# Weight sums of feed-forward groups 2 and 3: from beside group 1 into the second branch's projection

## The chip, the cores and the metric

One core of a Trainium2 chip runs the whole program. The metric is the device time of one execution in microseconds (us). TensorE (PE) multiplies, VectorE (DVE) and ScalarE (ACT) work on rows in on-chip memory, GpSimd (POOL) and SyncE (SP) issue transfers (DMAs) from queues of their own. The engines run side by side and wait for each other through semaphores.

## The reference

The reference is one block of a network on 256 tokens of width 2048, in 32-bit floats. What matters here, cut down:

```python
proj = x @ w_in                       # projections of both branches and two gates
o_a = gated_delta_rule_chunked(...)   # first branch
o_b = dsa_sparse_attention(...)       # second branch
merged = sigmoid(gate_a) * (o_a @ w_branch_a) + sigmoid(gate_b) * (o_b @ w_branch_b)
x = layer_norm(ALPHA * x + merged @ w_out)
h_gate, h_up = split(x @ w_ffn_in)    # 2048 x 11264
x = layer_norm(ALPHA * x + (silu(h_gate) * h_up) @ w_ffn_out)
```

## The kernel before

Every matrix product is made of three products of shortened numbers: a weight chunk of 128 x 1024 (512 KB) is loaded (`raw`), ACT makes its rounded part `hi` (L91), DVE the rest `lo = raw - hi` (L93), and `mm3` (L217 to L219) issues hi, lo and hi against the two parts of the activations, 512 columns each. `chunk` keeps four buffers each of `raw`, `hi` and `lo`.

Two K-tiles (a pair `q`) of a 1024-wide group of output columns form a 2 x 2 block product. `plain_pair` issues its 8 products (24 matmuls). `seven_pair` issues 7 (21 matmuls) in the manner of Strassen and Winograd: it needs sums of the activations (`f_form[q]`, made by `x_form`) and four sums of the weight blocks t1 to t4. Without prepared sums DVE makes them on the spot (`sum13`, L246; `sum24`, L250 and L251) and ACT and DVE split them (`thi`, `tlo`, L241 and L242). Where sums were prepared (`ready`), only one and a half chunks of the pair are left to load and split. After the last seven pair of a group, `sums_chain` (L1065 to L1072) reads the four shared accumulator banks (`wbank`) out, and the banks pass to the next group as its own four.

The first layers run in this order: projections, branch chains, `z_group`, four gate groups. Between the second and the third gate group stands the second branch's projection: four blocks of four chunks of `wbb`, twelve matmuls for each chunk. The feed-forward input layer is a first group 0 in two blocks (`wfi`) and ten groups of eight pairs (`x_group` on `wfg[i - 1]`, i from 1 to 10). `FQ[i - 1]` names the seven pairs of group i.

PE and SP run in program order. ACT, DVE and POOL are ordered by a scheduler from priorities: `high_priority(offset=LEAD)` moves work ahead, `offset=-LEAD` behind. Side work is written as generators ("chains"). `tick()` stands after each chunk or half pair and takes each chain to its next `yield`; the number yielded is how many ticks it rests. So a chain's SP transfers lie between the chunk loads of the tick in which they are issued.

Two chains prepare weight sums of pair 0 for the feed-forward groups:

- `kept_chain` (L941) makes those of groups 4 to 7 early in the program, with work behind everything else, writes them to DRAM (`d_s`) by POOL, and `kept_load` (L1407) brings each group's sums back while the group before it runs.
- the last part of `f_forms_chain` (L1385 on, `near`) makes those of groups 2 and 3 while group 1 starts, loads the raw weights, sums and splits them with ordinary priority, and keeps them on chip.

Group 1 itself has two seven pairs, 4 and 6, in the order 0 to 7. Groups 2 to 7 have four each, in the order `FO`.

Of the kernel before, what the change touches and what calls it, by code (L numbers as in the profile page):

```python
# [43 lines left out]
ZO = (0, 1, 3, 2, 4, 5, 6, 7)  # L44
OQ = (0, 2, 4, 6)
WALL = sorted({*WQ[0], *WQ[1]})
KEPT = (4, 5, 6, 7)
NEAR = (2, 3)
FQ = ((4, 6), *[(0, 2, 4, 6) if i in KEPT + NEAR else (2, 4, 6) for i in range(2, 11)])
FO = (1, 3, 2, 0, 4, 5, 6, 7)  # L50
KEPT_FROM = 56
OUT_AT = (8, 9, 10)
# [11 lines left out]
def block_kernel(ctx: ExitStack, tc: tile.TileContext, xT, x, cpack, onehot, relb, convw, alog, dtb, gnw,  # L64
# [35 lines left out]
    def start(gen, at_once=False):  # L100
        chains.append([gen, clock[0] + (next(gen) if at_once else 0)])
# [17 lines left out]
    def event(name):  # L119
        done[name] = clock[0]  # L120
# [86 lines left out]
    def split(hi, lo, src):  # L207
        nc.scalar.copy(hi, src)
        nc.vector.tensor_sub(lo, src, hi.bitcast(F32))
# [131 lines left out]
    def T(name, shape, dtype=F32, tag=None):  # L341
        return p1.tile(shape, dtype, name=name, tag=tag or name)
# [62 lines left out]
    def need(*names):  # L405
        for n in names:
            assert n in done, n
# [522 lines left out]
    def four_sums(ra, rb, lead=0):  # L930

        r0, r1, s0, s1 = (t[:, n * 512:n * 512 + 512] for t in (ra, rb) for n in range(2))
        with tc.high_priority(offset=lead):
            nc.vector.tensor_add(r0, r0, s1)
            nc.vector.tensor_add(s1, r1, s1)
        yield 1
        with tc.high_priority(offset=lead):
            nc.vector.tensor_add(r1, r0, r1)
            nc.vector.tensor_add(s0, r1, s0)

    def kept_chain():  # L941
        yield KEPT_FROM
        raws = [T("k_raw", [P, 2, 1024], tag=t) for t in ("oh_", "s_x")]
        hi = T("k_hi", [P, 2, 1024], F32R, tag="ol_")
        for m, g in enumerate(KEPT):
            raw = raws[m % 2]
            for i in range(2):
                nc.sync.dma_start(raw[:, i], wfg[g - 1, i])
                yield 1
            yield 1  # L950
            for _ in four_sums(raw[:, 0], raw[:, 1], -LEAD):
                yield 1
            yield 1
            for i in range(2):
                with tc.high_priority(offset=-LEAD):
                    for n in range(2):
                        cs = slice(n * 512, n * 512 + 512)
                        nc.scalar.copy(hi[:, i, cs], raw[:, i, cs])
                        nc.vector.tensor_sub(raw[:, i, cs].bitcast(F32R), raw[:, i, cs], hi[:, i, cs].bitcast(F32))
                yield 1  # L960
                nc.gpsimd.dma_start(d_s[m, 0, :, i], hi[:, i].bitcast(F32))
                nc.gpsimd.dma_start(d_s[m, 1, :, i], raw[:, i])
        event("kept")

    start(kept_chain())
    conv_first(s_kT, pss)
    event("kc0")
    for dst, h0, c0, ev in ((s_kT, 4, 12, "kc1"), (s_qT, 0, 0, "qc0"), (s_qT, 4, 4, "qc1"),
# [24 lines left out]
    def z_chain():  # L993

        yield "v1"
        yield 1
        need("kept")
        t0 = [rp.tile([P, 2, 1024], F32R, name=f"z_t{i}", tag=f"x1_{i}") for i in range(2)]
        wt = two("z_wt", F32, "ol_")
        gates_home.update(wraw=halves(two("z_wraw", F32, "oh_")), wt=halves(wt), thi=halves(t0[0]), tlo=halves(t0[1]))  # L1000
        for q, old in ((4, "s_ak"), (6, "s_sq")):
            t = T(f"g_form{q}", [P, 2, 4, P], F32R, tag=old)
            gates_form[q] = t[:, 0], t[:, 1]
        gates_form[2] = [p1.tile([P, 4, P], F32R, name="g_form2", tag="rel", bufs=2) for _ in range(2)]
        yield from early_sums(wz, ZQ[0], home, z_ready)
        yield 1
        x_form(ZQ[0], gates_form[ZQ[0]], wt[:, 0, :512], wt[:, 0, 512:])
        yield "lg"
        t1 = two("z_t2", F32R, "s_vT"), two("z_t3", F32R, "s_t")
        for tag, *t in zip(("thi", "tlo"), t0, t1):  # L1010
            gates_home[tag] = halves(*t)
            gates_home[tag][0] = 2
        yield from early_sums(wz, ZQ[1], home, z_ready)
        for q in ZQ[1:]:
            yield 1
            x_form(q, gates_form[q], wt[:, 0, :512], wt[:, 0, 512:])
        event("zready")
# [25 lines left out]
    def early_chain(src, qs, ready, ev):  # L1043
        for q in qs:
            yield from early_sums(src, q, home, ready)
        event(ev)

    def next_sets(*olds):
        for tag, old in zip(("thi", "tlo"), olds):
            e = gates_home[tag]  # L1050
            gates_home[tag] = [0, e[1][:2] + halves(two("h_" + old, F32R, old))[1]]
# [88 lines left out]

    def ga_rows():
        if "a" not in g_rows:
            next_sets("s_x", "s_mn")
            g_rows["a"] = [rp.tile([P, D], F32, name=f"ga{tb}", tag=f"x1_{tb}") for tb in range(NTB)]
        return g_rows["a"]
# [14 lines left out]
    for tag in ("thi", "tlo"):  # L1160
        gates_home[tag][0] = 0
    start(early_chain(wgt[2], (2, 4), ga_ready, "gaready"))
    for j in range(4):
        js = slice(j * 512, (j + 1) * 512)
        for tb, ps in enumerate(block_xs([wbb[j, k] for k in range(4)], *out_hl, ps_acc if j == 2 else ps_aux)):
            nc.vector.tensor_mul(gb[tb][:, js], ps, gb[tb][:, js])
# [72 lines left out]
    def h_tile(pool, i):  # L1239
        hH[i], hL[i] = (pool.tile([P, 4, S], F32R, name=f"{hl}{i}", tag=f"{hl}{i}") for hl in ("hH", "hL"))  # L1240
# [11 lines left out]
    def fetch(i, j):  # L1252
# [1 line left out]
        nc.sync.dma_start(t.rearrange("p k t -> p (k t)").bitcast(F32), d_h[i, j])  # L1254

    h_first = passing()
    near = [[hp_.tile([P, 1024], F32R if i > 1 else F32, name="near", tag=f"{hl}{i}") for hl in ("hH", "hL")]
            for i in range(1, 5)]
    l1 = ExitStack()
    gp = l1.enter_context(tc.tile_pool(name="gp1", bufs=1, side="left", reuse_waits="tile"))  # L1260
    ex = l1.enter_context(tc.tile_pool(name="ex1", bufs=4, side="left", reuse_waits="tile"))
# [93 lines left out]
                  lambda tb, ps: start(h_chain(0, tb, gated(tb, ps), ps_aux)))  # L1355
    l1.close()
    hp2 = fh.enter_context(tc.tile_pool(name="hp2", bufs=1, side="left", reuse_waits="tile"))
    near.append([hp2.tile([P, 1024], F32R, name="near", tag=f"{hl}5") for hl in ("hH", "hL")])
    kept = [None, [hp2.tile([P, 1024], F32R, name="kept", tag=f"{hl}6") for hl in ("hH", "hL")]]


    f_home = {}
# [13 lines left out]
    def f_forms_chain():  # L1376
        yield "x1"
        for tb in range(NTB):
            yield 2
            nc.sync.dma_start(d_x1[tb], x1[tb])  # L1380
        t = [rp.tile([P, 2, 2, 4, P], F32R, name="f_form", tag=f"x1_{tb}") for tb in range(NTB)]
        for i, q in enumerate((4, 6, 2, 0)):
            yield 1
            f_form[q] = t[i // 2][:, i % 2, 0], t[i // 2][:, i % 2, 1]
            x_form(q, f_form[q], fv(), fv())  # L1385
        yield 1
        raw = near[0]
        for m, g in enumerate(NEAR):
            for i in range(2):
                nc.sync.dma_start(raw[i], wfg[g - 1, i])  # L1390
                yield 1
            yield 1
            yield from four_sums(*raw)
            for i in range(2):
                yield 1
                split(near[1 + 2 * m][i], near[2 + 2 * m][i], raw[i])
            k_ready[g][0] = sums_of(near[1 + 2 * m], near[2 + 2 * m])
            yield 4

    k_ready = {g: {} for g in KEPT + NEAR}  # L1400

    def sums_of(hi, lo):
        (t1, t2), (t4, t3) = ([(hi[i][:, n * 512:n * 512 + 512], lo[i][:, n * 512:n * 512 + 512]) for n in range(2)]
# [3 lines left out]
    def kept_load(m):  # L1407

        for i in range(2):
            if m or not i:  # L1410
                kept[i] = [hp2.tile([P, 1024], F32R, name="kept", tag=f"{hl}{5 + i}") for hl in ("hH", "hL")]
            for j in range(2):
                if i or j:
                    yield 3
                nc.sync.dma_start(kept[i][j].bitcast(F32), d_s[m, j, :, i])
        k_ready[KEPT[m]][0] = sums_of(*zip(*kept))

# [47 lines left out]
    for i in range(1, NG + 1):  # L1465
        std, shared = (ps_aux, ps_acc) if i % 2 else (ps_acc, ps_aux)
        sums = []

        def places():
            sums.extend(fv() for _ in range(4))  # L1470
            return sums

        at = {6: lambda: start(kept_load(KEPT.index(i + 1)))} if i + 1 in KEPT else {}
        ready = k_ready.get(i)
        if ready is not None:
            at[0] = lambda ready=ready: ready[0]
        bank = x_group(wfg[i - 1], FQ[i - 1], std, shared, f_form, fhome, lambda wbank: sums_chain(places(), wbank),
                       at, range(8) if ready is None else FO, {} if ready is None else ready)
        if i == NEAR[-1]:
            for k in range(1, 5):  # L1480
                h_tile(hp_, k)
        if i == KEPT[-1]:
            for k in (5, 6):
                h_tile(hp2, k)
        if i == NG:
            h_tile(hp2, 7)
        start(hidden_chain(i, bank, sums, std), at_once=True)
# [258 lines left out]
```

## Time and profile before

| what | value |
|---|---|
| median of three runs (lowest, highest) | 1455.73 us (1454.38, 1456.3) |
| the profiled execution: its own time, its span | 1454.49 us, 1452.7 us |
| granted TensorE clock | 0.999 |
| PE, DVE, ACT busy, share of the span | 99%, 88%, 56% |
| moved from and to HBM | 312.88 MB read, 22.22 MB written |

The span goes from the first to the last instruction. A row of grouped instructions names the line, the engine, what is written and read, the count, the busy time and the mean time of one. A row of a tile gives minimum, median and maximum, and the first and the last start. In the timeline each row begins with the start and the duration in us, and a bracket gives the engine's idle time ahead of the instruction and what ended it. A matmul of 512 columns is shown as 0.39 us long, but they overlap: what counts is the distance between their starts.

### The profile page before, as it was taken

The page shows a single profiled execution, that of the slowest core. Times are in us where ns is not written, and L with a number is a line of the kernel's source. Part 1 is how long each engine was busy: PE and PEld are TensorE (multiplying, and loading weights), DVE is VectorE, ACT ScalarE, POOL GpSimd, SP SyncE. Part 2 cuts the span into 40 slices and gives each one's busy share as a digit, 9 for nine tenths or more (in the row PEclk, how much of TensorE's full clock was granted, in tenths as well). Part 3 has the DMA queues.
Part 4 walks back from the last instruction along what each step waited for, and adds up shares of the span by engine and source line. Part 5 has one row for each costly group of instructions (what it writes and reads, how often), then busy time and mean ns, then how long its engine had stood idle before and what let it go on. Part 6 is the DMA issues. An engine that isn't in the chain of part 4 may idle for free.

```text
span 1452.7 us, 19640 instructions
## 1 busy us (share of the span) xinstructions
PE 1443.7 (99%) x7140; PEld 1213.8 (84%) x7140; DVE 1279.0 (88%) x1763; ACT 813.9 (56%) x1021; POOL 56.2 (4%) x75
## 2 busy tenths in 40 slices
PE   9999999999999999999999999999999999999998
PEld 8888888888888888888888878888888888888887
DVE  6798988789699959998886999989999998989987
ACT  5765454557456646655435665656566565554552
POOL 0002011121000000000000000000000000000000
PEclk9999999999999999999999999999999999999999
DMA  8646589854556755756856767777766666887863
GB/s 293 197 159 196 175 216 335 295 187 151 169 198 232 233 193 198 247 188 204 304 202 218 264 236 253 251 271 255 279 211 212 216 215 247 311 342 265 315 215 118
DMA packets 101969, 336.40 MB, mean 232 GB/s; under 512 B 17696, under 2 KB 18888, under 8 KB 101360
## 3 DMA queue, kind: packets, MB, share of 16 engines
q1 hardware_dynamic: 88512, 310.03, 62.0%
q0 software_dynamic: 6176, 22.75, 4.6%
q10 hardware_dynamic: 7184, 2.36, 0.7%
q8 instruction: 56, 0.92, 0.2%
q14 instruction: 41, 0.34, 0.1%
HBM read 312.88 MB, written 22.22 MB: 231 GB/s over the span
## 4 chain that ended last, share of the span: by engine, by line
PE 92%; DVE 3%; DMA 3%; issue 1%; ACT 1%; SPq 0%; POOLq 0%; DVEq 0%; ACTq 0%
PE acc L217 10%; PE acc L218 10%; PE acc L219 10%; PE acc L153 10%; PE aux L218 9%; PE aux L217 9%; PE aux L219 9%; PE acc L156 5%; PE acc L175 3%; PE acc L173 3%; PE acc L174 3%; PE aux L173 2%; PE aux L174 1%; PE aux L175 1%; DMA raw<-in_win_dram 1%; PE aux L737 1%
## 5 line engine op out<-in xcount | busy, mean ns | idle before, releaser
L91 ACT CAST hi<-raw 128x1024 fp32r<-128x1024 f32 (+1 forms) x388 | 396.9, 1032 | 345.3 <-PE acc L219 87.3
L93 DVE TENSOR_TENSOR lo<-raw,hi 128x1024 fp32r<-128x1024 f32 (+1 forms) x388 | 463.5, 1205 | 87.3 <-ACT hi L91 84.7
L153 PE MATMUL acc<-X,hi 128*128 128x512 f32 x640 | 203.7, 400 | 0.0
L217 PE MATMUL acc<-hi,X 128*128 128x512 f32 x369 | 145.0, 393 | 0.8 <-DVE v L1072 0.8
L156 PEld LDWEIGHTS acc<-X,lo 128*128 128x128 f32 x640 | 120.2, 188 | 28.3
L219 PE MATMUL acc<-hi,X 128*128 128x512 f32 x369 | 143.7, 389 | 0.0
L218 PE MATMUL acc<-lo,X 128*128 128x512 f32 x369 | 143.6, 389 | 0.0
L156 PE MATMUL acc<-X,lo 128*128 128x256 f32 x640 | 126.0, 278 | 0.0
L217 PE MATMUL aux<-hi,X 128*128 128x512 f32 x313 | 122.4, 391 | 0.0
L219 PE MATMUL aux<-hi,X 128*128 128x512 f32 x313 | 121.9, 389 | 0.0
L218 PE MATMUL aux<-lo,X 128*128 128x512 f32 x313 | 121.8, 389 | 0.0
L153 PEld LDWEIGHTS acc<-X,hi 128*128 128x128 f32 x640 | 97.5, 189 | 2.0 <-ACT hi L91 0.7
L241 ACT CAST f_thi<-f_wt 128x1024 fp32r<-128x1024 f32 x58 | 61.0, 1053 | 46.4 <-DVE f_wt L251 23.9
L217 PEld LDWEIGHTS acc<-hi,X 128*128 128x128 f32 x369 | 69.3, 188 | 15.9 <-DVE v L1072 1.2
L219 PEld LDWEIGHTS acc<-hi,X 128*128 128x128 f32 x369 | 69.3, 188 | 14.5
L218 PEld LDWEIGHTS acc<-lo,X 128*128 128x128 f32 x369 | 69.3, 188 | 13.9
L242 DVE TENSOR_TENSOR f_tlo<-f_wt,f_thi 128x1024 fp32r<-128x1024 f32 x58 | 70.6, 1220 | 6.2 <-ACT f_thi L241 6.1
L219 PEld LDWEIGHTS aux<-hi,X 128*128 128x128 f32 x313 | 58.8, 188 | 12.3
L218 PEld LDWEIGHTS aux<-lo,X 128*128 128x128 f32 x313 | 58.8, 188 | 12.1
L217 PEld LDWEIGHTS aux<-hi,X 128*128 128x128 f32 x313 | 58.8, 188 | 12.0
L241 ACT CAST thi<-wt 128x1024 fp32r<-128x1024 f32 x36 | 37.9, 1054 | 49.0 <-DVE wt L246 31.6
L173 PE MATMUL acc<-hi,X 128*128 128x512 f32 x160 | 64.3, 402 | 0.0
(681 smaller groups left out, 3123.6 us busy)
## 6 DMA issues: line engine op xcount, KB each, us to landing
raw<-in_wfg_dram SPq DMA_DIRECT2D x125, 512.0 KB, 4.8
raw<-in_wws_dram SPq DMA_DIRECT2D x80, 512.0 KB, 4.1
raw<-in_wfo_dram SPq DMA_DIRECT2D x70, 512.0 KB, 5.0
raw<-in_wgt_dram SPq DMA_DIRECT2D x49, 512.0 KB, 3.9
f_wraw<-in_wfg_dram SPq DMA_DIRECT2D x29, 512.0 KB, 6.2
raw<-in_win_dram SPq DMA_DIRECT2D x21, 512.0 KB, 4.1
wraw<-in_wfo_dram SPq DMA_DIRECT2D x18, 512.0 KB, 5.1
gt<-d_g SPq DMA_DIRECT2D x18, 512.0 KB, 6.8
```

The source lines that it names most:

```text
L91: nc.scalar.copy(hi, raw)
L93: nc.vector.tensor_sub(lo, raw, hi.bitcast(F32))
L153: nc.tensor.matmul(pss[c], hv[:, kk, cs[c]], X2[k // 4][:, k % 4], start=(k == 0), stop=False, skip_group_check=True)
L156: nc.tensor.matmul(pss[c][:, :S], lv[:, kk, cs[c]], xh[:, k, :], start=False, stop=(k == KT - 1), skip_group_check=True)
L173: nc.tensor.matmul(ps, xh, hv[:, kk], start=(k == 0), stop=False)
L174: nc.tensor.matmul(ps, xh, lv[:, kk], start=False, stop=False)
L175: nc.tensor.matmul(ps, xl, hv[:, kk], start=False, stop=(k == 2 * n - 1))
L217: nc.tensor.matmul(o, sh, hi, start=first, stop=False)
L218: nc.tensor.matmul(o, sh, lo, start=False, stop=False)
L219: nc.tensor.matmul(o, sl, hi, start=False, stop=last)
L241: nc.scalar.copy(hi, v)
L242: nc.vector.tensor_sub(lo, v, hi.bitcast(F32))
```

## The change

`NEAR` goes; groups 2 and 3 join `KEPT`. `kept_chain` is started twice: for groups 4 to 7 as now, except that the list has become `range(2, 8)` and so the first start makes groups 2 to 5 (`m` from 0 to 3), and a second start makes groups 6 and 7 (`m` 4 and 5) in the second branch's projection. So six groups' sums go through `d_s`. The second start has one raw buffer (`s_x`), puts the rounded part into `s_rv`, and rests 5 ticks between its two groups. `kept_load` now brings in groups 2 to 7, the first during group 1. The `near` part of `f_forms_chain` and its tiles go. Group 1 gets pair 2 as a third seven pair and the order `F1`.

```diff
-KEPT = (4, 5, 6, 7)
-NEAR = (2, 3)
-FQ = ((4, 6), *[(0, 2, 4, 6) if i in KEPT + NEAR else (2, 4, 6) for i in range(2, 11)])
+KEPT = range(2, 8)
+FQ = [(0, 2, 4, 6) if i in KEPT else (2, 4, 6) for i in range(1, 11)]
+F1 = (1, 3, 4, 5, 6, 0, 2, 7)
...
-    def kept_chain():
-        yield KEPT_FROM
-        raws = [T("k_raw", [P, 2, 1024], tag=t) for t in ("oh_", "s_x")]
-        hi = T("k_hi", [P, 2, 1024], F32R, tag="ol_")
-        for m, g in enumerate(KEPT):
-            raw = raws[m % 2]
+    def kept_chain(ms, wait, old, old_hi, gap, ev):
+        yield wait
+        raws = [T(f"k_raw{t}", [P, 2, 1024], tag=t) for t in old]
+        hi = T(f"k_hi{old_hi}", [P, 2, 1024], F32R, tag=old_hi)
+        for m in ms:
+            if gap and m > ms[0]:
+                yield gap
+            raw = raws[m % len(old)]
             for i in range(2):
-                nc.sync.dma_start(raw[:, i], wfg[g - 1, i])
+                nc.sync.dma_start(raw[:, i], wfg[KEPT[m] - 1, i])
...
-    start(kept_chain())
+    start(kept_chain(range(4), KEPT_FROM, ("oh_", "s_x"), "ol_", 0, "kept0"))
...
     start(early_chain(wgt[2], (2, 4), ga_ready, "gaready"))
+    start(kept_chain(range(4, 6), 1, ("s_x",), "s_rv", 5, "kept1"))
...
-    near = [[hp_.tile([P, 1024], F32R if i > 1 else F32, name="near", tag=f"{hl}{i}") for hl in ("hH", "hL")]
-            for i in range(1, 5)]
+    for i in range(1, 5):
+        h_tile(hp_, i)
...
-        raw = near[0]
-        for m, g in enumerate(NEAR):
-            for i in range(2):
-                nc.sync.dma_start(raw[i], wfg[g - 1, i])
-                yield 1
-            yield 1
-            yield from four_sums(*raw)
-            for i in range(2):
-                yield 1
-                split(near[1 + 2 * m][i], near[2 + 2 * m][i], raw[i])
-            k_ready[g][0] = sums_of(near[1 + 2 * m], near[2 + 2 * m])
-            yield 4
...
         bank = x_group(wfg[i - 1], FQ[i - 1], std, shared, f_form, fhome, lambda wbank: sums_chain(places(), wbank),
-                       at, range(8) if ready is None else FO, {} if ready is None else ready)
+                       at, F1 if i == 1 else range(8) if ready is None else FO, {} if ready is None else ready)
```

The check that the sums have been written moves too: what follows in the first branch needs `kept0`, the third gate group's rows need `kept1`.

More of the change, by code (lines that the diff above doesn't have):

```diff
@@ L962, in kept_chain @@
                 nc.gpsimd.dma_start(d_s[m, 1, :, i], raw[:, i])
-        event("kept")
-    start(kept_chain())
+        event(ev)
+    start(kept_chain(range(4), KEPT_FROM, ("oh_", "s_x"), "ol_", 0, "kept0"))
     conv_first(s_kT, pss)
@@ L996, in z_chain @@
         yield 1
-        need("kept")
+        need("kept0")
         t0 = [rp.tile([P, 2, 1024], F32R, name=f"z_t{i}", tag=f"x1_{i}") for i in range(2)]
@@ L1142, in ga_rows @@
         if "a" not in g_rows:
+            need("kept1")
             next_sets("s_x", "s_mn")
@@ L1357, in block_kernel @@
     hp2 = fh.enter_context(tc.tile_pool(name="hp2", bufs=1, side="left", reuse_waits="tile"))
-    near.append([hp2.tile([P, 1024], F32R, name="near", tag=f"{hl}5") for hl in ("hH", "hL")])
-    kept = [None, [hp2.tile([P, 1024], F32R, name="kept", tag=f"{hl}6") for hl in ("hH", "hL")]]
+    kept = [[hp2.tile([P, 1024], F32R, name="kept", tag=f"{hl}{5 + i}") for hl in ("hH", "hL")] for i in range(2)]
     f_home = {}
@@ L1385, in f_forms_chain @@
             x_form(q, f_form[q], fv(), fv())
-        yield 1
-        raw = near[0]
-        for m, g in enumerate(NEAR):
-            for i in range(2):
-                nc.sync.dma_start(raw[i], wfg[g - 1, i])
-                yield 1
-            yield 1
-            yield from four_sums(*raw)
-            for i in range(2):
-                yield 1
-                split(near[1 + 2 * m][i], near[2 + 2 * m][i], raw[i])
-            k_ready[g][0] = sums_of(near[1 + 2 * m], near[2 + 2 * m])
-            yield 4
-    k_ready = {g: {} for g in KEPT + NEAR}
+    k_ready = {g: {} for g in KEPT}
     def sums_of(hi, lo):
@@ L1409, in kept_load @@
         for i in range(2):
-            if m or not i:
+            if m:
                 kept[i] = [hp2.tile([P, 1024], F32R, name="kept", tag=f"{hl}{5 + i}") for hl in ("hH", "hL")]
@@ L1477, in block_kernel @@
         bank = x_group(wfg[i - 1], FQ[i - 1], std, shared, f_form, fhome, lambda wbank: sums_chain(places(), wbank),
-                       at, range(8) if ready is None else FO, {} if ready is None else ready)
-        if i == NEAR[-1]:
-            for k in range(1, 5):
-                h_tile(hp_, k)
+                       at, F1 if i == 1 else range(8) if ready is None else FO, {} if ready is None else ready)
         if i == KEPT[-1]:
```

## The prediction

> **What bounds the kernel now.** I read the page first, then what the weight loads waited for around group 1, then the timeline there.
>
> ```profile
> span 1452.7 us, 19640 instructions
> ...
> PE 1443.7 (99%) x7140; PEld 1213.8 (84%) x7140; DVE 1279.0 (88%) x1763; ACT 813.9 (56%) x1021; POOL 56.2 (4%) x75
> ```
>
> TensorE never rests for long, so a change can gain only what it takes out of TensorE's own list of matmuls, and what it takes out of the few waits that TensorE has. Between 790 and 842 us there are two, both at the step from group 1 to group 2 (who waited for whom: total, times, longest):
>
> ```profile
> PEld acc L217 <- DVE v L1072: 1.2, 1, 1.2
> PEld acc L217 <- DVE v L1071: 0.4, 1, 0.4
> ```
>
> The timeline of PE there, and of DVE just before:
>
> ```profile
> 836.62 0.39 PE L217 MATMUL acc<-hi,X 128*128 128x512 f32 x1
> 836.85 0.39 PE L218 MATMUL acc<-lo,X 128*128 128x512 f32 x1
> 837.07 0.39 PE L219 MATMUL acc<-hi,X 128*128 128x512 f32 x1
> 837.47 0.50 PE L217 MATMUL acc<-hi,X 128*128 128x512 f32 x1
> 837.81 0.39 PE L218 MATMUL acc<-lo,X 128*128 128x512 f32 x1
> 838.04 0.40 PE L219 MATMUL acc<-hi,X 128*128 128x512 f32 x1
> 839.21 0.50 PE L217 MATMUL acc<-hi,X 128*128 128x512 f32 x1 [0.78 <-DVE v L1072]
> 839.54 0.39 PE L218 MATMUL acc<-lo,X 128*128 128x512 f32 x1
> ```
>
> ```profile
> 832.67 1.22 DVE L209 TENSOR_TENSOR near<-near 128x1024 fp32r<-128x1024 f32 x1
> 833.81 0.68 DVE L1067 TENSOR_TENSOR v<-v,acc 128x512 f32<-128x512 f32 x1
> 834.40 1.22 DVE L209 TENSOR_TENSOR near<-near 128x1024 fp32r<-128x1024 f32 x1
> ```
>
> Undisturbed, matmuls start 0.227 us apart (836.62 to 837.07 is two steps). From 837.07 to 839.54 there are five steps in 2.47 us where 5 x 0.227 = 1.13 would do: 1.33 us lost. The reader sees why: group 2 gets its four accumulator banks from group 1's `sums_chain`, and in DVE's queue that chain stands between the last splits of `near`. These are what the change takes away.
>
> Here are the stages concerned: the branch projection (the first two rows), a stretch of the early `kept_chain`, group 1 and group 2. The columns are us, then each engine's busy time, PEclk, DMA share, GB/s.
>
> ```profile
> 470.00:505.00 35.00, 35.00 (x156) 28.99 (x155) 34.62 (x39) 22.38 (x26) 0.00 (x0) 1.00 0.74 243
> 505.00:530.00 25.00, 25.00 (x112) 20.70 (x111) 13.99 (x15) 9.49 (x9) 0.00 (x0) 1.00 0.61 191
> 216.70:247.70 31.00, 31.00 (x226) 27.23 (x225) 28.34 (x52) 15.24 (x23) 4.34 (x8) 1.00 0.93 318
> 797.00:838.00 41.00, 40.99 (x183) 33.67 (x182) 40.93 (x54) 25.79 (x31) 1.13 (x2) 1.00 0.78 265
> 838.00:880.00 42.00, 41.23 (x186) 33.88 (x185) 41.65 (x51) 24.82 (x31) 2.12 (x4) 1.00 0.71 243
> ```
>
> **The third seven pair.** 21 matmuls in place of 24: 3 x 0.227 = 0.68 us off TensorE, certain, since nothing else is issued for it there. On DVE it costs more. Its rows in group 1:
>
> ```profile
> L93 DVE TENSOR_TENSOR lo<-raw,hi 128x1024 fp32r<-128x1024 f32 x12 | 14.5, 1219 | 0.0
> L209 DVE TENSOR_TENSOR near<-near 128x1024 fp32r<-128x1024 f32 x4 | 4.9, 1220 | 0.0
> L242 DVE TENSOR_TENSOR f_tlo<-f_wt,f_thi 128x1024 fp32r<-128x1024 f32 x4 | 4.9, 1220 | 0.0
> L242 DVE TENSOR_TENSOR lo<-f_wraw,hi 128x1024 fp32r<-128x1024 f32 x2 | 2.4, 1218 | 0.0
> L246 DVE TENSOR_TENSOR f_wt<-f_wraw,raw 128x1024 f32<-128x1024 f32 x2 | 2.4, 1218 | 0.0
> ```
>
> Half-wide operations take 0.685 us (a row on `k_raw` below). A plain pair is two L93, 2.44 us. A seven pair is one full and one half split, the sum L246, two half sums and two L242: 1.22 + 0.69 + 1.22 + 1.37 + 2.44 = 6.94. That is 4.5 us more.
>
> **The `near` work taken out of group 1.** Eight half sums (four for each of two groups) and four splits: 8 x 0.69 + 4 x 1.22 = 10.4 us of DVE, and as many loads as `kept_load` now brings for group 2 (four of 512 KB). DVE comes out 5.9 us lighter, about 35 of 41 us against 40.93. Group 2 shows that this is enough: it has four seven pairs and DVE at 41.65 of 42, and what PE lacks there (42.00 - 41.23) is the 0.78 of the wait at 839.21, so there is no wait at its own end. The last seven pair stays the seventh of eight pairs, in `F1` as in the old order, so `sums_chain` has the same one plain pair (24 x 0.227 = 5.4 us) to pass the banks on. I therefore take the whole 1.33 us as gained; the bounds are 0 and 1.33. Pair 4 comes two pairs earlier in `F1`; its activation sums are the first of four, ready at 779.9, ahead of group 1, and DVE's relief lies just there, so nothing for that:
>
> ```profile
> L209 DVE TENSOR_TENSOR f_form<-v,f_form x4: 684/685/687, 779.2 to 812.1; 128x512 fp32r<-128x512 f32 x4
> ```
>
>
> **The second start of `kept_chain`.** For each of two groups: two loads by SP, four half sums and four half splits on DVE (8 x 0.69 = 5.5 us), four half casts on ACT, four writes by POOL. DVE is full until 505 and 56% busy after; ACT has room and POOL nothing else to issue (0.00 in both rows); TensorE has none of this work. DMA gains 2.1 MB of loads and 4.2 MB of writes. On top of 243 GB/s x 35 and 191 x 25 (13.3 MB) that makes 19.6 MB in 60 us, 326 GB/s if all of it fell in there; the 216.7 row ran 318 GB/s at share 0.93, 342 when full, with PE at 31.00 of 31. So bandwidth costs nothing. In group 2, 243 GB/s and 2.1 MB for group 3's sums make 293, under the same row: nothing.
>
> What can cost is SP's order. The single raw buffer's second load, for the next group, stands in SP's queue between chunks 13 and 14 of `wbb`, and can't start before the first group's raw half has been written out by POOL. Behind it wait chunks 14 and 15 and all of the third gate group's. (The other half's load follows one chunk later, and its write is one tick later too.) The rows: SP's issue of chunks 1 to 3 and of chunk 13; the landing of the `wbb` chunks; PE's start on chunk 0; ACT's cast; a gap of DVE after 505.
>
> ```profile
> 474.67 2.56 SPq L89 DMA_DIRECT2D raw<-in_wbb_dram  x3
> ```
> ```profile
> 505.34 0.33 SPq L89 DMA_DIRECT2D raw<-in_wbb_dram x1
> ```
> ```profile
> DMA to landing us min/median/max: 3.5/4.3/5.3
> ```
> ```profile
> L173 PE MATMUL aux<-hi,oh__3751 x48: 389/389/389, 486.4 to 529.3; 128*128 128x512 f32 x48
> ```
> ```profile
> L91 ACT CAST hi<-raw 128x1024 fp32r<-128x1024 f32 x12 | 12.3, 1048 | 1.3 <-PE aux L219 1.2
> ```
> ```profile
> 514.92 1.22 DVE L93 TENSOR_TENSOR lo<-raw,hi 128x1024 fp32r<-128x1024 f32 x1 [1.49 <-ACT hi L91]
> ```
>
> TensorE needs chunk 14 at 486.4 + 14 x 12 x 0.227 = 524.5. A load, a cast and a split before that (4.3 + 1.05 + 1.22) it must be issued: 517.9. SP comes to the second load at 505.7. So the hold is free up to 12.2 us, and after that TensorE stands still for as long. How long one round takes, from the load to the write, I take from the early chain: its tile's rows, the second round's load and write, and the landing of writes to `d_s`.
>
> ```profile
> L959 DVE TENSOR_TENSOR k_raw<-k_raw,k_hi x16: 664/682/691, 226.2 to 281.9; 128x512 fp32r<-128x512 f32 x16
> L948 SPq DMA_DIRECT2D k_raw<-in_wfg_dram x8: 383/458/655, 189.4 to 268.3; - x8
> L962 POOL DMA_DIRECT2D d_s<-k_raw x8: 531/533/559, 231.9 to 282.9; - x8
> L934 DVE TENSOR_TENSOR k_raw<-k_raw x4: 672/685/693, 206.6 to 274.2; 128x512 f32<-128x512 f32 x4
> ```
> ```profile
> 216.71 0.42 SPq L948 DMA_DIRECT2D k_raw<-in_wfg_dram  x1
> ```
> ```profile
> 240.88 0.53 POOL L962 DMA_DIRECT2D d_s<-k_raw  x1 [2.09 <-DVE k_raw L959]
> ```
> ```profile
> DMA to landing us min/median/max: 3.0/6.7/8.4
> ```
>
> The first round took 231.9 - 189.4 = 42.5 us to the write, the second 24.2; with 6.7 for the landing, 49.2 and 30.9. The load behind chunk 1 goes out at about 475.1, so the raw half is free between 506.0 and 524.3. The cost lies between 0 and 524.3 - 517.9 = 6.4 us. The second round is the nearer row: DVE was 91% busy in it, and here 99% for 30 us and then half free. Even the middle of both, 515, is under the limit, so I take 0 and keep 6.4 for the range.
>
> [...]
>
> **The sum.** -0.68 - 1.33 + 0 = -2.0 us: a span of 1450.7, and 1454.49 - 2.0 = 1452.5 for the profiled execution. That one lies 1.2 us under the median of the runs shown, so the median becomes 1455.73 - 2.0 = 1453.7, -0.14%. What a measurement of this kernel can tell from no change is about 0.2%, 2.9 us.
>
> **The rivals.** *SP held too long (the other side).* DVE has only gaps of 1.49 us for each chunk from 505 on. If the low-priority work gets nothing else, its first six operations (two and two sums, two splits; 4.1 us) fill three gaps and end at 514.9; with 0.53 for the issue and 6.7 the half is free at 522.1. Chunk 14 is then 4.2 us late: 1453.7 + 4.2 = 1457.9. It decides from 519.9 on, where the stall eats the 2.0 us. For it speaks DVE's 34.62 of 35 us; against it the second round. Of the way from 506.0 to 524.3, 35% lies past 517.9, 24% past 519.9 and 8% past 522.8 (slower by over 0.2%). Chance 0.25.
>
> *The wait at group 2 stays.* The third seven pair's work has high priority and now stands right ahead of `sums_chain`, where `near` stood. Against it: pair 6 stood there before, and group 2 has the same order without a wait. Then only 0.68 is gained: 1455.05. Chance 0.1.
>
> *More is gained than the list shows.* PE is at 35.00 of 35 and 25.00 of 25 in the projection, so there is nothing to gain there; a faster time by over 0.2% would be the scatter of the runs (1454.38 to 1456.3) on top of the forecast. Chance 0.05.
>
> **How the numbers follow.** The forecast has 0.6. Its own range is the forecast and half the scatter of the runs, 1452.7 to 1454.7. Towards slower I go to the rival's 1457.9, towards faster to 1452.2 (half the scatter and a half us more, for the order that the scheduler makes anew on DVE and ACT). Faster by over 0.2%: 0.05 of the third rival, and a quarter of the forecast, which lies 0.9 us from that border: 0.2. Slower: 0.1 of the first rival, and 0.03 for a wait that no row here shows: 0.13. Within: 0.67.
>
> **What the next profile would show.** Right: 7137 matmuls; no wait on L1071 or L1072 ahead of group 2, DVE with gaps in group 1; PE without a gap between 480 and 545; SP's wait for `d_s` ahead of the second load under 12 us. Wrong: a gap of PE at about 524 to 530 on a `wbb` chunk, released by a load; or the two waits again, behind splits of pair 2. The prediction fails most easily on where the scheduler puts the low-priority work on DVE between 475 and 515.

## The result, and the profile after

| kernel | median (lowest, highest) | profiled execution: time, span | clock |
|---|---|---|---|
| before, six runs | 1454.66 us (1453.72, 1456.3) | 1454.49, 1452.7 | 0.999 |
| after, six runs | 1462.63 us (1459.38, 1465.03) | 1462.83, 1461.0 | 0.996 |

The ratio of after to before is 1.0053, with an interval of 1.0039 to 1.0067: 8 us slower, where I had forecast 2 us faster, and outside my range. The page of the changed kernel, in the lines that answer to those of before:

```profile
span 1461.0 us, 19681 instructions
...
PE 1447.4 (99%) x7137; PEld 1216.3 (83%) x7137; DVE 1284.2 (88%) x1772; ACT 816.1 (56%) x1027; POOL 60.3 (4%) x83
```

The 21 matmuls in place of 24 are there (7137), and yet PE is busy 3.7 us longer. So some matmuls got longer, and the span grew by more than that. (Some 1.7 us of the longer busy time belong to the program's start, below.) What the weight loads waited for between 790 and 842 us (total, times, longest):

```profile
PEld acc L217 <- issue: 4.8, 1, 4.8
```

and what the matmuls waited for between 805 and 817:

```profile
PE acc L217 <- DVE pass L209: 4.4, 1, 4.4
```

The two waits on L1071 and L1072 at the step to group 2 are gone, as forecast. One wait has taken their place, in the middle of group 1, and it isn't one of those that I had listed. PE's timeline there, then DVE's:

```profile
811.10 0.39 PE L219 MATMUL acc<-f_thi,f_form 128*128 128x512 f32 x1
815.94 0.76 PE L217 MATMUL acc<-f_thi,f_form 128*128 128x512 f32 x1 [4.45 <-DVE pass L209]
816.50 0.63 PE L218 MATMUL acc<-f_tlo,f_form 128*128 128x512 f32 x1
816.93 0.63 PE L219 MATMUL acc<-f_thi,f_form 128*128 128x512 f32 x1
817.35 0.63 PE L217 MATMUL aux<-f_thi,X 128*128 128x512 f32 x1
...
821.19 0.41 PE L217 MATMUL aux<-hi,X 128*128 128x512 f32 x1
```

```profile
812.43 0.69 DVE L209 TENSOR_TENSOR f_form<-v,f_form 128x512 fp32r<-128x512 f32 x1
813.03 1.22 DVE L242 TENSOR_TENSOR lo<-f_wraw,hi 128x1024 fp32r<-128x1024 f32 x1
814.17 0.69 DVE L242 TENSOR_TENSOR lo<-raw,hi 128x512 fp32r<-128x512 f32 x1
814.77 0.68 DVE L250 TENSOR_TENSOR f_wt<-f_wt,f_wraw 128x512 f32<-128x512 f32 x1
815.37 0.42 DVE L209 TENSOR_TENSOR pass<-acc,pass 128x256 fp32r<-128x256 f32 x1
```

Two losses stand in the first of these. From 811.10 to 815.94 TensorE takes one step of 0.227 us and stands for the other 4.61. Then twelve steps, 815.94 to 821.19, take 5.25 us where 12 x 0.227 = 2.72 would do: 2.53 us more. The table by stretches says why (us, busy time of PE, PEld, DVE, ACT and POOL, then PEclk, the share of the DMA engines and GB/s):

```profile
797.00:811.00 14.00, 14.00 (x65) 11.59 (x65) 14.00 (x25) 8.89 (x13) 0.58 (x1) 1.00 0.65 221
811.00:816.00 5.00, 0.55 (x4) 0.16 (x2) 5.00 (x8) 2.31 (x3) 0.00 (x0) 0.84 0.99 387
816.00:821.20 5.20, 5.20 (x13) 4.03 (x14) 5.10 (x6) 2.10 (x2) 0.55 (x1) 0.50 0.74 247
821.20:841.00 19.80, 19.80 (x89) 16.35 (x88) 11.91 (x12) 9.79 (x11) 0.00 (x0) 1.00 0.55 189
```

After the standstill the granted clock is 0.50, and the same number of matmuls takes nearly twice as long. PE counts as busy there, which is one reason why its busy time rose though it had fewer matmuls. Here the 0.50 followed a standstill of 4.61 us; near the program's start (below) the same profile has 0.50 after one of only 1.67 us. The last section comes back to this.

The wait is for `pass`, in `h_chain`. Its last split (L208 on ACT, L209 on DVE) reads group 0's second transposed block out of shared accumulator banks, at ordinary priority. A seven pair needs those four banks (`wbank`). In the order `F1` group 1's first seven pair is the third pair, in the old order the fifth. DVE's rows of these two reads, before and then after:

```profile
L209 DVE TENSOR_TENSOR pass<-acc,pass x2: 418/420/421, 807.2 to 809.3; 128x256 fp32r<-128x256 f32 x2
```

```profile
L209 DVE TENSOR_TENSOR pass<-acc,pass x2: 418/418/418, 809.6 to 815.4; 128x256 fp32r<-128x256 f32 x2
```

The second read is 6.1 us later. The changed kernel comes to this place 1.7 and 1.5 us later anyway (both below), so 2.9 of these are its own: the operations shown ahead of it, a split of `f_form` and pair 6's splits and sums with LEAD priority, now come before it. The bank that it frees (`wbank[1]`) is wanted by the third of the seven pair's products of weight sums, the one that stood still above; in the kernel before that product starts at

```profile
818.94 0.39 PE L217 MATMUL acc<-f_thi,f_form 128*128 128x512 f32 x1
```

and in the changed one a step after 811.10. So before there were 818.94 - 809.3 - 0.42 = 9.2 us to spare. Two pairs are 48 steps, 10.9 us; the reordering alone turns the 9.2 into -1.7, and the read's own 2.9 make it -4.6, the standstill.

Elsewhere, in the old kernel the weight loads waited 0.2 us on `ga` in all between 520 and 600 us. Now they wait so:

```profile
PEld aux L217 <- DVE ga L1074: 0.8, 1, 0.8
PEld acc L217 <- DVE ga L1115: 0.7, 1, 0.7
PEld aux L174 <- DVE lo L93: 0.4, 1, 0.4
PEld acc L217 <- issue: 0.3, 1, 0.3
```

By the distances of the matmuls these cost 0.28 at 528, 0.62 at 576 and 0.57 at 584: 1.47 us. Both profiled executions run the same instructions up to the projection, whose first matmul starts at 486.43 before and 488.13 after. That difference of 1.7 us arises at the program's start. The first matmul on `wsh` starts at 12.34 before and at 14.31 after: from 8.82 to 12.24 us the changed kernel's profile has a granted clock of 0.50, the old one's 1.00. (Over all the kernels below, with the same work up to there, the projection's first matmul lies between 485.90 and 488.15.) From this matmul to the end the span grew by 972.87 - 966.27 = 6.60 us, and the parts add up: -0.68 - 1.33 + 4.61 + 2.53 + 1.47 = 6.60.

### The profile page after: what moved, and what is told of

It is laid out like the page before. It is cut to its first block, busy times and chain, and to the rows that moved or that the text cites. A ratio compares the mean times of both kernels' runs of the same rounds, so it can differ in the third digit from the quotient of the medians.

```text
span 1461.0 us, 19681 instructions
## 1 busy us (share of the span) xinstructions
PE 1447.4 (99%) x7137; PEld 1216.3 (83%) x7137; DVE 1284.2 (88%) x1772; ACT 816.1 (56%) x1027; POOL 60.3 (4%) x83
## 4 chain that ended last, share of the span: by engine, by line
PE 70%; DVE 3%; DMA 1%; issue 1%; ACT 0%; POOLq 0%; DVEq 0%; ACTq 0%
PE acc L217 10%; PE acc L218 10%; PE acc L219 10%; PE aux L219 9%; PE aux L217 9%; PE aux L218 9%; PE acc L175 2%; PE acc L173 2%; PE acc L174 2%; PE aux L174 2%; PE aux L175 1%; PE aux L173 1%; DMA raw<-in_wgt_dram 1%; DVE lo L93 1%; DVE lo L242 1%
## 5 line engine op out<-in xcount | busy, mean ns | idle before, releaser
L217 PE MATMUL aux<-hi,X 128*128 128x512 f32 x306 | 120.3, 393 | 0.3 <-DVE ga L1074 0.3
L219 PE MATMUL aux<-hi,X 128*128 128x512 f32 x306 | 119.6, 391 | 0.0
```

What stands on the lines that cost most here:

```text
L217: nc.tensor.matmul(o, sh, hi, start=first, stop=False)
L219: nc.tensor.matmul(o, sl, hi, start=False, stop=last)
```

## The experiments

The theory: `F1` takes a bank that `h_chain`'s low-priority read still holds, and the standstill halves the clock (0.50 in the table above). The rivals: the kept sums themselves (SP's hold, DVE's extra work) make it slow; or the third seven pair does, by its work on DVE. Each run's ratio is to the kernel before, measured in the same session.

**The first seven pair late again (e1), the read first (e2), the move alone (e3), the third pair alone (e4).** Beside them in the same runs before had 1454.68.

```diff
e1   -F1 = (1, 3, 4, 5, 6, 0, 2, 7)
     +F1 = (1, 3, 5, 0, 4, 6, 2, 7)
e2   -        split(h_first[0][:, fs, ts], h_first[1][:, fs, ts], a[:, ...])
     +        with tc.high_priority(offset=LEAD):
     +            split(h_first[0][:, fs, ts], h_first[1][:, fs, ts], a[:, ...])
e3   changed kernel, but FQ[0] = (4, 6) and F1 = range(8)
e4   kernel before, but FQ[0] = (2, 4, 6) and F1 = (1, 3, 4, 5, 6, 0, 2, 7)
```

> The changed kernel with group 1's three seven pairs at the fifth, sixth and seventh place (order 1, 3, 5, 0, 4, 6, 2, 7) in place of the third, fifth and seventh. Bank theory (the first seven pair asks for four shared banks two pairs too early, while one still holds a transposed block that VectorE reads late): no gap ahead of group 1's first seven pair, no matmuls 0.43 us apart, time 1462.6 - 7.3 = about 1455.3. Sums theory (VectorE is late with the weight sums of the first seven pair): the same, about 1455.3. Move theory (the loads of kept sums in group 1 or the early work in the projection cost the time): gap stays, 1460 or more.

> The changed kernel with one thing changed: the split of group 0's transposed second blocks, which frees the accumulator banks, gets the priority of the chunk work on ScalarE and VectorE. Order F1 stays. Bank theory: the wait of 4.8 us shrinks under 1.5 us and the slow matmuls after it go, time 1455.3 to 1457. Sums theory: the first seven pair still waits as long, 1461 to 1463. Move theory: as after, 1461 to 1463.

> The move alone: the changed kernel with group 1's two seven pairs (4 and 6) and the order 0 to 7 as before. Bank and sums theory: no gap in group 1 and none at its end, so 1454.7 - 1.3 plus some 1.5 us lost in the projection and the gate groups: 1454.5 to 1456. Move theory: 1460 or more.

> The third seven pair alone: the kernel before with pair 2 as a third seven pair and the order F1 in group 1, sums of groups 2 and 3 still made beside group 1. Bank and sums theory: the gap ahead of the first seven pair is there, at least as long as with the move since VectorE has 10.4 us more to do: 1461 to 1466. Move theory: no gap there, 1454.

e1 gave 1454.84, ratio to before 0.9999 (0.999 to 1.0008): 7.8 us come back through the order alone, with all the kept sums and the third seven pair in place. e2 keeps `F1` and only lets the read go first: 1455.46, ratio 1.0007 (0.9998 to 1.0016). In neither is there a wait row between 790 and 842. e2's two reads and its stretch of the old standstill:

```profile
L209 DVE TENSOR_TENSOR pass<-acc,pass x2: 415/416/418, 806.7 to 807.1; 128x256 fp32r<-128x256 f32 x2
```

```profile
811.00:816.00 5.00, 5.00 (x24) 4.14 (x23) 5.00 (x11) 1.17 (x3) 0.00 (x0) 1.00 1.02 387
```

DVE is as full as in the changed kernel (5.00 of 5) and TensorE doesn't miss a step. So in the changed kernel it wasn't the amount of DVE's work, but what stood ahead of one operation of 0.42 us.

e3, the move without `F1` and without the third pair, gave 1455.72, 1.0009 (1.0 to 1.0017): the move alone costs no 8 us, but it doesn't bring the 1.33 us either. e4, the third pair and `F1` without the move, gave 1464.64, 1.0067 (1.0053 to 1.0081). Its wait, and the two stretches:

```profile
PEld acc L218 <- issue: 7.4, 2, 4.3
```

```profile
807.00:812.00 5.00, 1.08 (x6) 0.61 (x5) 5.00 (x12) 3.12 (x5) 0.58 (x1) 0.81 0.78 257
812.00:820.20 8.20, 5.81 (x13) 4.09 (x14) 8.20 (x11) 3.57 (x4) 0.55 (x1) 0.50 0.44 170
```

Here `near`'s work still fills DVE, both reads are late (811.3 and 815.3), TensorE stands 4.08 and then 2.79 us, and runs at 0.50. The order makes the loss in either kernel; the work moved away makes it smaller.

**How far back is enough (e9).** The first seven pair in fourth place, one pair later than in the change.

```diff
-F1 = (1, 3, 4, 5, 6, 0, 2, 7)
+F1 = (1, 3, 5, 4, 6, 0, 2, 7)
```

> The changed kernel with the seven pairs at the fourth, fifth and seventh place of group 1 (order 1, 3, 5, 4, 6, 0, 2, 7), one plain pair (5.4 us) later than in F1. Bank theory: TensorE asks for the fourth shared bank at 811.3 + 5.4 = 816.7 by the changed kernel's times, and VectorE gave it up at 815.8 there, so the wait of 4.8 us falls to 0 to 1 us and no matmuls are slow: 1455 to 1456.5. If the wait were made of work that any first seven pair brings on VectorE, it would move along and stay at 3 us or more: 1459 or more.

1455.6, 1.0007 (0.9997 to 1.0017). What is left of the wait between 790 and 842, and the two reads:

```profile
PEld acc L217 <- issue: 0.3, 1, 0.3
```

```profile
L209 DVE TENSOR_TENSOR pass<-acc,pass x2: 411/412/412, 813.6 to 815.7; 128x256 fp32r<-128x256 f32 x2
```

The second read is as late as in the change (815.7 to 815.4), and costs next to nothing: the bank is wanted one pair, 5.4 us, later. The lateness itself was harmless; the place of the pair in the order made it count.

**The standstill filled with work (e5).** In front of the product that waits, the one before it is issued seven times more, so 21 matmuls that change nothing in the result.

```diff
         mm3(wbank[3], *form(0), *t1, first, last)
+        for _ in range(fill):        # 7 in group 1's first seven pair
+            mm3(wbank[2], *form(2), *t3, True, True)
```

> The changed kernel with its order F1; ahead of the matmuls that wait for the fourth shared bank, TensorE repeats three products of the same first seven pair into a bank that is open anyway seven times (21 matmuls, 4.8 us; the real ones then begin that bank anew). The wait itself is not shortened. Clock theory (TensorE stands idle for over 4 us, and for the 5 us after that its matmuls start 0.43 us apart in place of 0.227, which costs some 2.4 us more): the matmuls after the filling start 0.227 us apart, time 1462.6 - 2.4 = 1460.2. Without such an effect (the slow matmuls come from something else, such as late data or a busy memory): they stay slow, 1462 to 1463.

1460.56, 1.0042 (1.0028 to 1.0055), 2.1 us less than the change. Its stretches beside those of the change:

```profile
811.00:816.00 5.00, 5.00 (x23) 4.14 (x23) 4.93 (x7) 2.09 (x3) 0.10 (x1) 1.00 0.99 324
816.00:821.20 5.20, 5.20 (x24) 4.30 (x24) 2.33 (x3) 1.06 (x1) 0.00 (x0) 1.00 0.77 290
```

21 x 0.227 = 4.77 us of useless work in place of 4.61 of standing, and 24 matmuls in the next 5.2 us in place of 13. So the half clock follows from the standing, and is worth about the 2.53 us that I had counted. The scheduler also moved the second read (to 809.8), ahead of the time at which the bank is wanted. So this run says nothing about the bank, and the matmuls were added to a kernel without the wait. Beside e2, where the read is early too, 4.77 us of useless work cost 5.1 us (1460.56 to 1455.46); in the change 4.61 us of standing cost 7.14.

**What keeps e1 from being faster than before (e6, e7).** e1 has the -0.68 and the -1.33 and is no faster; it loses about 1.6 us at 575, 583 and 528. Either SP's hold does it (SP waits 12.4 us for `d_s` in the change), or the second round's work, on DVE and in transfers, which reaches into the third gate group. e6 lets the second round start three ticks later, so that SP should find the buffer free; e7 leaves the second round out (group 7 then has three seven pairs, which TensorE pays with 0.68 us).

```diff
e6   e1 and  -start(kept_chain(range(4, 6), 1, ("s_x",), "s_rv", 5, "kept1"))
             +start(kept_chain(range(4, 6), 1, ("s_x",), "s_rv", 8, "kept1"))
e7   e1 and  -KEPT = range(2, 8)
             +KEPT = range(2, 7)
             -start(kept_chain(range(4, 6), 1, ("s_x",), "s_rv", 5, "kept1"))
             +start(kept_chain(range(4, 5), 1, ("s_x",), "s_rv", 5, "kept1"))
```

> The late order of seven pairs (e1), and in the projection a rest of 8 ticks between the two rounds of kept sums in place of 5. In e1 TensorE still loses about 0.3 us at 528 and 1.4 us at 575 and 583, at the end of the third gate group. Hold theory (SyncE's 10 us hold uses up the lead of the loads, and the gate group never wins it back): no hold, both losses go, 1453.1. Work theory (the second round's work on VectorE and its transfers fall into the gate group, which has them to spare no more): only the 0.3 us go, the loss at 575 and 583 stays or grows, 1454.5 to 1457.

> The late order (e1) with kept sums for groups 2 to 6 alone: one round in the projection, and group 7 has three seven pairs in place of four (0.68 us more on TensorE). Work theory and hold theory: the losses at 528, 575 and 583 go, 1454.8 + 0.7 - 1.7 = 1453.8. If neither, that is if the losses come from the first round or from the moved queue order: 1455.5.

e6: 1458.26, 1.0022 (1.0012 to 1.0032). SP's wait fell, and the waits for `ga` grew. The waits in SP's queue, then those of the weight loads between 520 and 600 (the longest three):

```profile
SPq L950 <- DMA d_s<-k_raws_x: 5.5, 2, 3.6
```

```profile
PEld aux L217 <- DVE ga L1073: 1.6, 1, 1.6
PEld aux L217 <- DVE ga L1074: 1.2, 1, 1.2
PEld acc L217 <- DVE ga L1115: 0.7, 1, 0.7
```

So less hold, more loss: the length of the hold doesn't set it. It isn't a clean test, though. SP still waited 5.5 us, now among the third gate group's loads, and the time lies above the 1454.5 to 1457 expected for the work theory. e7: 1453.75, 0.9991 (0.9983 to 1.0), and in the same stretch only

```profile
PEld acc L217 <- DVE ga L1115: 0.2, 1, 0.2
```

The link is a weight sum of the third gate group, which waits for its own load. DVE's timeline, in the change and in e7:

```profile
548.77 1.23 DVE L246 TENSOR_TENSOR g_wt<-g_wraw,raw 128x1024 f32<-128x1024 f32 x1 [2.57 <-DMA raw<-in_wgt_dram]
```

```profile
545.47 1.23 DVE L246 TENSOR_TENSOR g_wt<-g_wraw,raw 128x1024 f32<-128x1024 f32 x1 [0.95 <-DMA raw<-in_wgt_dram]
```

DVE waited there 0.98 us in the kernel before, 0.95 in e7, 2.57 in the change, 3.75 in e3 and 4.21 in e6. DVE comes out of it later, and with it, by the waits listed above, `sums_chain` of that group, which hands its banks on late (L1073, L1074, L1115).

The traces tell how that load (L282) is late. The times of issue are counted from the projection's first matmul; the shares are those of the DMA engines between 535 and 545 us.

| kernel | issued after | landed in | DMA share, GB/s |
|---|---|---|---|
| before | 55.1 us | 3.5 us | 0.67, 232 |
| e7 | 55.1 us | 3.5 us | 0.66, 219 |
| change | 55.5 us | 5.1 us | 0.92, 332 |
| e6 | 56.8 us | 6.0 us | 0.98, 331 |

In the change it goes out 0.3 us later and then takes 1.6 us longer to land. So the larger part of the delay arises between issue and landing, while the DMA engines are fuller than before, and the smaller part in SP's order. Whether the second round's own transfers fill them or the loads that SP catches up with after its hold, no run separates.

e7 is the best version that I ran. Its span is 1451.8, its matmuls are 7140, and it has the 1.33 us of the change. Its median lies 1.2 us below that of before, but its interval reaches 1.0, so a gain isn't shown.

**The late order without the move (e8).** `near` stays beside group 1, with the third seven pair in e1's order.

```diff
-FQ = ((4, 6), ...
+FQ = ((2, 4, 6), ...
+F1 = (1, 3, 5, 0, 4, 6, 2, 7)
```

> The kernel before (sums of groups 2 and 3 made beside group 1) with the third seven pair in the late order of e1. Bank theory: no gap of 4 us ahead of the first seven pair and no slow matmuls, so far faster than the 1464.6 of the early order; VectorE has 4.5 us more in a group where it was 100% busy, so the wait at group 1's end grows by up to 4.5 us: 1454 to 1459. Sums theory: the gap stays at 4 us or more, 1460 or more.

1460.3, 1.0045 (1.0032 to 1.0057): more than I had thought. The bank's wait is gone (reads at 805.9 and 807.9), but TensorE now waits for sums, and 5.3 us go to one kind of wait. The first row lies in group 1, the second in group 2 (873 to 877 us):

```profile
PEld acc L219 <- DVE f_tlo L243: 3.0, 3, 2.1
PEld aux L219 <- DVE f_tlo L243: 2.3, 4, 1.3
```

```profile
825.00:835.00 10.00, 7.63 (x31) 5.41 (x30) 10.00 (x12) 5.21 (x6) 0.00 (x0) 1.00 0.59 217
```

With both pieces of work beside group 1 DVE can't keep up. So the move does make room for the third seven pair, as the prediction worked out: e1, which has it, shows no wait in this group. The longest standstill here, 2.04 us (a matmul at 829.47, the next at 831.74, less 0.227), left the clock at 1.00.

## Why the prediction was wrong

**The step that failed** is the sentence in the part on `near`: "Pair 4 comes two pairs earlier in `F1`; its activation sums are the first of four, ready at 779.9 ... so nothing for that." I asked whether the pair's *data* were ready, and they were. I didn't ask who still held the *banks* that it writes. The row that would have told, the tile `pass` with DVE's reads at 807.2 and 809.3, the prediction doesn't show. The bank had 9.2 us to spare and two pairs took 10.9, and its reader, at ordinary priority, fell behind LEAD work. That step was put at 0 and measured 7.14 us (4.61 of standing, 2.53 of slow clock).

**"DVE's relief lies just there"** failed as well. The relief is real, but it comes after pair 6's sums: in the table above DVE is at 14.00 of 14, 5.00 of 5 and 5.10 of 5.2, and only from 821 on at 11.91 of 19.8. I had divided the saving by the whole of group 1.

**The third seven pair** was right: 7137 matmuls. Its cost on DVE was covered in e1: no wait shows in group 1 there.

**The wait at group 2** was right: gone, in the change and in e1, with the same one plain pair ahead of it.

**The second start of `kept_chain`** was right in its mechanism and a little off in size. SP waited and then issued chunk 14 in the changed kernel so (SP's waits, its timeline):

```profile
SPq L950 <- DMA d_s<-k_raws_x: 12.4, 2, 9.8
```

```profile
517.27 0.33 SPq L950 DMA_DIRECT2D k_raws_x<-in_wfg_dram  x1
517.69 0.42 SPq L89 DMA_DIRECT2D raw<-in_wbb_dram  x1
```

I had bounded the free buffer by 506.0 and 524.3 and put chunk 14's limit at 517.9 by the old kernel's clock, 519.6 in this execution, which reached the projection 1.7 us later. Chunk 14 went out at 517.69, in time. The write that freed the buffer was issued at 514.3 and SP went on at 517.27, 3.0 us later: the landing of 6.7 us that the prediction went by was too long here (the five writes to `d_s` issued between 505 and 530 us landed in 2.9 to 4.0). The 0.28 us that TensorE lost at 528.93 are on chunk 15: the prediction named the other half's load ahead of it and gave it no cost. Chunk 15 went out at 521.16 and landed 4.7 us later, and its cast on ACT (526.52) and its split on DVE (528.05) each stood behind an operation of the second round. So of the rival "SP held too long" a fifteenth of its price came, one chunk further on.

**"So bandwidth costs nothing"** failed too, further on. I had put all the new transfers between 470 and 530 us and let the second round end with the projection. In fact they reach into the third gate group: from 535 to 545 us the change moved 332 GB/s, 232 before, and the load above landed in 5.1 us in place of 3.5. TensorE lost 1.2 us in that group in the change, 1.4 in e1 and more in e3 and e6; this alone would have taken more than half of the 2.0 us forecast.

**The rivals "more is gained" and "the wait stays"** didn't happen. None of the three named the bank that `h_chain` still holds.

## What to carry over

When products are reordered, list what each *writes* as well as what it reads: ask of every shared accumulator who reads it last, at what priority, and when, and compare that with the new time of need. A cheap operation at ordinary priority that frees a bank should have the priority of whoever waits for the bank (e2: one line, 7.2 us). Price a standstill of TensorE of several us at more than its length, since the matmuls behind it may be slow (the change: 4.61 us of standing cost 7.14). And when work is moved to a stage, look at the stage after it too, at its transfers as well as its engines.

## What the runs showed of the hardware

The twelve matmuls of the slow stretch in the change started 0.43 us apart in place of 0.227, and full speed came back after 5.25 us, at 2.53 us of extra time. That a stall of 4.6 us costs 7.1 in all I hadn't expected.

In these runs the length of a standstill alone doesn't tell whether the clock falls. 2.04 us (e8) left it at 1.00; 4.08 us (e4, 4.3 in its row of waits) and 4.61 us (the change) brought it to 0.50. But near the start of the changed kernel 0.50 (from 8.82 to 12.24 us) followed a longest standstill of 1.67 us (one matmul at 6.12, the next at 7.91, 0.12 apart when undisturbed). The kernel before stands 1.34 us at that place (5.97 and 7.43) and stays at 1.00. What decides beside the length, no run here separates.
